# A two-layer hybrid encoder on one core: both directions of the delta rule in one step with unscaled keys, the decay tables moved to the v and q convolutions, and the inversion's columns on one engine

## The chip, the core and the metric

One Trainium2 core: TensorE (PE in the profile) multiplies matrices, VectorE (DVE), ScalarE (ACT) and GpSimd (POOL) work on rows, and SyncE's queue (SP) issues nearly all DMAs. Everything is float32. The metric is the device time of one execution in microseconds; lower is better.

## The reference, cut to what matters

Two layers act on 1024 tokens of width 1024. Each layer normalises the tokens, projects them with one matrix of 3376 columns, runs three mixers (gated linear attention, the gated delta rule, cross-attention into a memory of 256 tokens), gates them, and projects back. The change is about the delta rule: 4 heads of width 96, chunks of 64 tokens, 16 chunks, once from left to right and once from right to left with gates of its own; the two results are added.

```python
def _gated_delta_chunked(q, k, v, g, beta):
    gc = jnp.cumsum(g, axis=-1)
    diff = gc[..., :, None] - gc[..., None, :]
    decay = jnp.where(incl, jnp.exp(jnp.where(incl, diff, 0.0)), 0.0)
    kk = jnp.einsum('bhncd,bhnsd->bhncs', k, k)
    a_strict = jnp.where(strict, kk * decay * beta[..., :, None], 0.0)
    t_mat = a_strict + jnp.eye(c, dtype=jnp.float32)
    rhs = jnp.concatenate([v * beta[..., None], k * (beta * jnp.exp(gc))[..., None]], axis=-1)
    sol = lax.linalg.triangular_solve(t_mat, rhs, left_side=True, lower=True, unit_diagonal=True)
    u, w = sol[..., :dv], sol[..., dv:]
    qk = jnp.where(incl, jnp.einsum('bhncd,bhnsd->bhncs', q, k) * decay, 0.0)
    q_dec = q * jnp.exp(gc)[..., None]
    k_to_end = k * jnp.exp(gc[..., -1:] - gc)[..., None]
    chunk_decay = jnp.exp(gc[..., -1])
    def step(s, inp):
        u_c, w_c, q_c, qk_c, k_c, dec_c = inp
        v_new = u_c - jnp.einsum('bhcd,bhdv->bhcv', w_c, s)
        o = jnp.einsum('bhcd,bhdv->bhcv', q_c, s) + jnp.einsum('bhcs,bhsv->bhcv', qk_c, v_new)
        s = dec_c[..., None, None] * s + jnp.einsum('bhcd,bhcv->bhdv', k_c, v_new)
        return s, o
```

With M for the inverse of `t_mat` (with beta folded in), u is M·v and w is M·(exp(gc)·k). So v_new = u − w·S can also be had as M·(v − exp(gc)·(k·S)); the change rests on that identity.

## The kernel before, in words

A layer has three phases. **phase_norm** normalises eight tiles of 128 tokens, transposes them, and multiplies the first columns of the in-projection. **phase_proj** multiplies the others, tile by tile of 128 output columns ("dense": pieces of 6 matmuls `mm<-Hh,wh` and the like, 128x512, on numbers split into a high and a low part), and starts the delta rule with what comes out: three k convolutions, then three v, then three q (`conv_sink`, four 128x1024 multiply-adds each on DVE, line 535), L2 norms, transposes back, the decay tables N (`decays`, per head: a subtraction on POOL, a minimum on DVE, an exponential on ACT), the products q·k and k·k (`phase_a`), and the inverse M (`invert`: a column-by-column elimination of 32x32 blocks, in columns 0 to 29 on DVE and in columns 30 and 31, as X2, on POOL). Dense pieces are pulled in between (`pull`, `upto`).

**phase_mix** runs the recurrence (`chain`), and after each of its yields lets `filler` issue other work for some nanoseconds of a budget (FILL): the gates and states of the linear attention (`gla_pre`, PE tile `x`), what is left of dense, units of the mixers (`x`, `ga`, `gb`), loads of the output weights (`load_wout`: `wor`, split on ACT and DVE at line 1522), and output tiles.

Before, the chain prepares each tile of two chunks per direction: it scales keys twice on POOL (`ke`, `kend`), builds block-diagonal copies of M on ACT (`Mb`), forms u and w with 8 matmuls (PE tile `pt`) and evacuates both. A chunk step then takes 4 matmuls for w·S and q·S together (`cp<-S,wq`, M=128), DVE's `vn`, 4 matmuls for the state (`R<-vn,kend`), DVE's addition to `S·dec` (POOL), and the outputs (`cp<-vn,qkt`, both directions in turn), which ACT copies out and POOL adds. The backward direction runs one piece behind the forward one. The scaled queries are made in phase_proj (`row`, POOL, lines of phase_proj) and stored in `qd_d`.

PE's instructions are pinned to the order of the code. The other engines' order is a scheduler's, and each of them works through its list in that order, so an instruction that waits holds back all behind it.

## Time and profile before

| | us |
|---|---|
| median of three runs (lowest, highest) | 1391.71 (1391.15, 1397.26) |
| the profiled execution, its own time | 1387.57 |
| its span, first to last instruction | 1385.8 |
| PE busy | 1260.7 (91%) |
| DVE busy | 814.8 (59%) |
| ACT busy | 655.5 (47%) |
| POOL busy | 549.6 (40%) |
| mean granted TensorE clock | 0.965 of full speed |

The profiled execution has 1.8 us outside its span, and the median of the runs lies 4.1 us above it. A fp32 matmul is two records in the trace, so "x8" in a row of the chain is four matmuls. Where a row names a helper's line (84, 87, 90, 98, 101), go by the tile: all matmuls have line 98, all DVE tensor-tensor operations line 87. The stage of the chain lies at 353 to 583 us in layer 0 and at 1041 to 1272 us in layer 1; the convolutions are at 85 to 245 and 765 to 925, the inversions at 262 to 350 and 942 to 1040.

### The profile page before, as it was taken

To read this page: it belongs to the slowest core of one execution; us is meant where nothing else is said; L and a number is where in the kernel's file an instruction comes from. 1 tells how busy PE (TensorE), PEld (TensorE's weight loads), DVE (VectorE), ACT (ScalarE), POOL (GpSimd) and SP (SyncE) were. 2 spreads that over 40 slices of the span, in tenths; PEclk is the share of its full clock that TensorE was granted. 3 is DMA by queue.
4 is the path that set the end of the run, shared out by engine and by line. 5 is a ranking of instruction groups with operands and counts; after the bars stand their busy time and mean duration, and the time that the engine had idled before them with its cause. 6 is when DMAs were issued, how large, how long until landed. Compare 5 with 4: busy or idle time off the path is not lost. (4 is left out here: it accounts for less than half of the span.)

```text
span 1385.8 us, 24239 instructions
## 1 busy us (share of the span) xinstructions
PE 1260.7 (91%) x9482; PEld 1047.5 (76%) x9482; DVE 814.8 (59%) x1163; ACT 655.5 (47%) x1373; POOL 549.6 (40%) x579
## 2 busy tenths in 40 slices
PE   6998799987999988999999988996978998999997
PEld 5986688776777777887788766884767787778886
DVE  5336855498377557356272578455865784564553
ACT  5335564162766655233262545531637675543432
POOL 4026434576534544211310454444854445432111
PEclk9999999999999999999999999998999999999999
DMA  7161234752686865244652413257427776642532
GB/s 223 57 134 35 74 91 130 245 157 69 187 242 197 236 192 144 81 145 125 188 169 66 107 46 106 61 158 221 136 66 225 210 229 203 205 130 80 161 103 106
DMA packets 247857, 198.99 MB, mean 144 GB/s; under 512 B 68032, under 2 KB 215936, under 8 KB 247744
## 3 DMA queue, kind: packets, MB, share of 16 engines
q1 hardware_dynamic: 245584, 189.59, 47.2%
q10 hardware_dynamic: 2016, 7.34, 1.5%
q8 instruction: 75, 1.23, 0.4%
q0 software_dynamic: 144, 0.52, 0.1%
q14 instruction: 38, 0.31, 0.1%
HBM read 138.82 MB, written 58.59 MB: 142 GB/s over the span
## 5 line engine op out<-in xcount | busy, mean ns | idle before, releaser
L98 PE MATMUL mm<-Hh,wh 128*128 128x512 f32 x736 | 311.8, 424 | 31.7 <-ACT acc L84 15.9
L98 PE MATMUL mm<-Hh,wl 128*128 128x512 f32 x736 | 295.9, 402 | 0.0
L98 PE MATMUL mm<-Hl,wh 128*128 128x512 f32 x736 | 295.6, 402 | 0.0
L90 POOL TENSOR_TENSOR wl<-wr,wh 128x1024 fp32r<-128x1024 f32 x46 | 119.4, 2596 | 211.0 <-ACT wh L84 188.3
L98 PEld LDWEIGHTS mm<-Hh,wh 128*128 128x128 f32 x736 | 143.5, 195 | 66.7 <-ACT acc L84 19.3
L535 DVE SCALAR_TENSOR_TENSOR acc<-pad,convw,acc 128x1024 f32<-128x1024 f32 x72 | 139.9, 1943 | 66.4 <-ACT acc L84 63.8
L98 PEld LDWEIGHTS mm<-Hh,wl 128*128 128x128 f32 x736 | 143.2, 195 | 32.3
L98 PE MATMUL mm<-wo,oh 128*128 128x512 f32 x512 | 167.1, 407 | 0.2 <-DVE xr L87 0.2
L98 PEld LDWEIGHTS mm<-Hl,wh 128*128 128x128 f32 x736 | 144.2, 196 | 26.0
L90 POOL TENSOR_TENSOR ol<-z,oh 128x512 fp32r<-128x512 f32 x32 | 41.2, 1286 | 163.6 <-ACT oh L84 161.4
L98 PEld LDWEIGHTS mm<-wo,oh 128*128 128x128 f32 x512 | 90.3, 189 | 17.8 <-issue 0.8
L98 PE MATMUL mm<-wo,ol 128*128 128x512 f32 x256 | 101.2, 395 | 0.0
L90 POOL TENSOR_TENSOR S<-S,dec 96x384 f32<-96x384 f32 x56 | 55.5, 991 | 87.4 <-DVE S L87 66.9
L90 POOL TENSOR_TENSOR acc<-acc,pad 128x1024 f32<-128x1024 f32 x18 | 45.6, 2531 | 107.8 <-ACT pad L84 107.8
L84 ACT ACTIVATE wh<-wr 128x1024 fp32r<-128x1024 f32 x46 | 48.4, 1053 | 74.8 <-PE mm L98 66.2
L98 PEld LDWEIGHTS cp<-S,wq 96*128 96x128 f32 x480 | 62.7, 197 | 14.9 <-ACT oa L84 6.4
L98 PE MATMUL cp<-S,wq 96*128 96x96 f32 x480 | 65.1, 280 | 9.2 <-ACT oa L84 5.5
L84 ACT ACTIVATE oh<-z 128x512 fp32r<-128x512 f32 x32 | 20.2, 632 | 80.4 <-DVE z L87 80.3
L87 DVE TENSOR_TENSOR vn<-u,cp 64x384 f32<-64x384 f32 x60 | 33.0, 550 | 40.9 <-PE cp L98 33.4
L98 PEld LDWEIGHTS mm<-wo,ol 128*128 128x128 f32 x256 | 48.1, 188 | 11.5
L90 POOL TENSOR_TENSOR sp<-sp,sg 128x512 f32<-128x512 f32 x32 | 45.3, 1417 | 28.8 <-ACT sg L84 17.6
L90 POOL TENSOR_TENSOR row<-row,qT 96x1024 f32<-96x1024 f32 x16 | 38.0, 2383 | 44.0 <-DMA row<-row_d 29.3
(311 smaller groups left out, 2652.1 us busy)
## 6 DMA issues: line engine op xcount, KB each, us to landing
wr<-in_w_in_dram SPq DMA_DIRECT2D x46, 512.0 KB, 4.0
kv<-kv_d SPq DMA_DIRECT2D x32, 384.0 KB, 4.4
zT<-sp SPq DMA_DIRECT2D x32, 256.0 KB, 2.4
ge_d<-qe SPq DMA_DIRECT2D x32, 256.0 KB, 3.7
wor<-in_w_out_dram SPq DMA_DIRECT2D x16, 512.0 KB, 4.6
gqk<-ge_d SPq DMA_DIRECT2D x16, 512.0 KB, 4.0
z<-zT SPq DMA_DIRECT2D x16, 512.0 KB, 4.5
row<-row_d SPq DMA_DIRECT2D x16, 384.0 KB, 6.3
```

The lines of the kernel that those rows point to most:

```text
L84: return self.nc.scalar.activation(out, in_, func, **kw)
L87: return self.nc.vector.tensor_tensor(out, a, b, op=op)
L90: return self.nc.gpsimd.tensor_tensor(out, a, b, op=op)
L98: return self.pin(self.nc.tensor.matmul(*args, **kw))
L535: nc.vector.scalar_tensor_tensor(acc, pad[:, j:j + T], self.convw[:, f, j:j + 1], acc, op0=ALU.mult, op1=ALU.add)
```

## The change

The recurrence takes the same chunk step of both directions at once. A step loads keys and queries 96 wide by 64 tokens (`kq`), a broadcast row of exp(gc) (`row`), keys and values in token rows (`kv`) and the q·k block (`qk`), two steps ahead, in 8 DMAs. It multiplies the unscaled keys and the scaled queries with S (8 matmuls each, 64 output rows a piece), forms X = v − exp(gc)·(k·S) on DVE in four operations, multiplies M by X (8 matmuls, 64x64), copies the result out (`vn`, ACT) and scales it for the state (`ve`, DVE), multiplies it by the unscaled keys (`R`, 8 matmuls) and adds. Outputs are copied by ACT in the first half of the steps and added by DVE from PSUM in the second. `ke`, `kend`, `Mb`, u, w, their evacuations and the store `qd_d` are gone; queries are scaled per step on POOL (96x2x256). Three of the four decay tables move from the k to the v and q convolutions. All 32 columns of the inversion are on DVE. Constants of the fill change, and `left` counts what dense has left in place of an estimate.

```diff
-FILL = 1200
-FILL2 = 1200
-FILLW = 1200
-FILL3 = 1200
+FILL = 1950
+FILL2 = 1950
+FILLW = 1950
+FILL3 = 1950
-PRE_D = 24
+PRE_D = 32
-INV = 6000
-DC0 = 0
-CUT = 30
+INV = 9000
-DEN0 = 3
+DEN0 = 6
...
@@ phase_proj
-        self.qd_d = self.DR.tile([2, HD, 4, T], F32, tag="qdd", name="qd_d")
+        self.kq_d = self.DR.tile([HD, 2, 4, T], F32, tag="kqd", name="kq_d")
...
             self.conv_t(3 + i, k_tok[:, :, i * 128:i * 128 + 128])
-            if i >= DC0:
-                next(dec, None)
...
                     self.back_t(k_tok, h, kT[h])
+                    nc.sync.dma_start(self.kq_d[:, 0, h], kT[h])
...
             self.conv_t(i, q_tok[:, :, i * 128:i * 128 + 128])
-        for _ in dec:
-            pass
+            next(dec, None)
...
             self.back_t(q_tok, h, qT[:, h, :])
-            for d in range(2):
-                row = ST.tile([P, T], F32, tag="acc", name="row", bufs=3)[0:HD]
-                nc.sync.dma_start(row.rearrange("p (t c) -> p t c", t=NT),
-                                  self.row_d[:, d * 4 + h].unsqueeze(0).to_broadcast([HD, NT, P]))
-                self.ptt(row, row, qT[:, h, :], ALU.mult)
-                nc.sync.dma_start(self.qd_d[d, :, h], row)
+            nc.sync.dma_start(self.kq_d[:, 1, h], qT[:, h, :])
@@ invert
-            self.ptt(tv, U[:, :, 0:j, j:j + 1].to_broadcast(sh), X2[:, :, j:j + 1, c0:].to_broadcast(sh), ALU.mult)
-            self.ptt(X2[:, :, 0:j, c0:], X2[:, :, 0:j, c0:], tv, ALU.subtract)
-        for j in range(CUT - 1, 0, -1):
-            w = CUT - j
+            w = 32 - j
...
-        self.act(X[:, :, :, CUT:], X2)
@@ phase_mix, filler
-        closePX = self.psum(cp=2, R=1, pt=1, x=2)
+        closePX = self.psum(cp=2, R=2, x=2)
...
-        left = (23 - self.tiles) * 8 - 2
+        left = self.left
...
-            while busy and done < units * left // MIXN:
+            while busy and (done < units * left // MIXN or units >= MIXU):
@@ chain
+    def chain_load(self, MP, n):
+        kv = MP.tile([P, 2, 4, HD], F32, tag="kv", name="kv", bufs=3)
+        kq = MP.tile([HD, 2, 2, 4, 64], F32, tag="kq", name="kq", bufs=3)
+        row = MP.tile([HD, 2, 4, 64], F32, tag="row", name="row", bufs=2)
+        qk = MP.tile([P, 4, 64], F32, tag="qk", name="qkt", bufs=3)
+        for d in range(2):
+            t, f, r = self.place(d, n)
+            cs = slice(t * 128 + f * 64, t * 128 + f * 64 + 64)
+            nc.sync.dma_start(kq[:, d].rearrange("p e h c -> p (e h) c"),
+                              self.kq_d[:, :, :, cs].rearrange("p e h c -> p (e h) c"))
+            nc.sync.dma_start(row[:, d], self.row_d[t, d * 4:d * 4 + 4, f * 64:f * 64 + 64]
+                              .unsqueeze(0).to_broadcast([HD, 4, 64]))
+            nc.sync.dma_start(kv[r].rearrange("p k h d -> p k (h d)"), self.kv_d[:, t, r].rearrange("k p c -> p k c"))
+            nc.sync.dma_start(qk[r], self.qkd[:, r, t, d, :].rearrange("h p c -> p h c"))
...
+            if n:
+                ks = self.ps("cp", [P, 4, HD])
+                for e, to in ((0, ks), (1, o)):
+                    for h in range(4):
+                        for d in range(2):
+                            self.mat(to[at[d][2], h, :], p["kq"][:, d, e, h, :], S[d][:, h, :],
+                                     start=h == 0, stop=e == 0 and h == 3, skip_group_check=True)
+                    if e == 0:
+                        X = MP.tile([P, 4, HD], F32, tag="X", name="X", bufs=1)
+                        for h in range(4):
+                            self.nc.vector.scalar_tensor_tensor(X[:, h, :], ks[:, h, :], neg[:, n, h:h + 1], x[:, h, :],
+                                                                op0=ALU.mult, op1=ALU.add)
+                        x = X
+                if n < N2 - 1:
+                    for d in range(2):
+                        new[d] = MP.tile([HD, 4, HD], F32, tag=f"S{d}", name=f"S{d}", bufs=2)
+                        dec = self.dec[0:HD, at[d][1], at[d][0], d * 4:d * 4 + 4]
+                        self.ptt(new[d], S[d], dec.unsqueeze(2).to_broadcast([HD, 4, HD]), ALU.mult)
+                yield
+            pv = self.ps("R", [P, 4, HD])
+            for h in range(4):
+                for d, (t, f, r) in enumerate(at):
+                    self.mat(pv[r, h, :], self.M[d][r, h, t, :], x[r, h, :], start=True, stop=True)
+            vn = MP.tile([P, 4, HD], F32, tag="vn", name="vn", bufs=1)
+            self.act(vn, pv)
+            ve = MP.tile([P, 4, HD], F32, tag="ve", name="ve", bufs=1)
+            self.tt(ve, pv, end[:, n].unsqueeze(2).to_broadcast([P, 4, HD]), ALU.mult)
+            if n + 1 < N2:
+                self.chain_scale(n + 1, loads[n + 1])
+            yield
+            if n < N2 - 1:
+                R = [self.ps("R", [P, 4, HD]) for _ in range(2)]
+                for h in range(4):
+                    for d, (t, f, r) in enumerate(at):
+                        self.mat(R[d][0:HD, h, :], p["kv"][r, 0, h, :], ve[r, h, :], start=True, stop=True)
...
+                        self.tt(new[d], R[d][0:HD], new[d], ALU.add)
+            for h in range(4):
+                for d, (t, f, r) in enumerate(at):
+                    self.mat(o[r, h, :], p["qk"][r, h, :], vn[r, h, :],
+                             start=n == 0 and h == 0, stop=h == 3, skip_group_check=True)
...
+            if n + 2 < N2:
+                loads[n + 2] = self.chain_load(MP, n + 2)
+            yield
```

How this moves instructions is seen at three places. The first is PE in layer 0, within the chain, while dense pieces are still there. Before (`R` is the state update of one direction, `pt` the w unit, `x` a transpose for the linear attention, `cp<-vn,qkt` the outputs of both):

```order
L98 MATMUL mm<-Hl_106,wh 128x512
L98 MATMUL mm<-Hh_105,wl 128x512
L98 MATMUL R<-vn,kend 96x96 x4
L98 MATMUL pt<-Mb_3165,ke 96x128 x4
L101 MATMUL x<-ident,qe 128x128 x4
L98 MATMUL R<-vn,kend 96x96 x4
L98 MATMUL cp<-vn,qkt 64x96 x8
L98 MATMUL pt<-kv,Mb_3166 128x96 x4
L98 MATMUL mm<-Hh_107,wh 128x512
```

After, at the same dense piece:

```order
L96 MATMUL mm<-Hl_106,wh 128x512
L96 MATMUL mm<-Hh_105,wl 128x512
L96 MATMUL R<-ve,kv 96x96 x8
L96 MATMUL cp<-vn,qkt 64x96 x8
L99 MATMUL x<-ident,qe 128x128 x4
L96 MATMUL mm<-Hh_107,wh 128x512
L96 MATMUL mm<-Hl_108,wh 128x512
L96 MATMUL mm<-Hh_107,wl 128x512
L96 MATMUL mm<-Hh_107,wh 128x512
L96 MATMUL mm<-Hl_108,wh 128x512
L96 MATMUL mm<-Hh_107,wl 128x512
L96 MATMUL cp<-S_3296,kq 64x96
```

The two state updates stand in one group, the `pt` units are gone, and between the update and the next product with S stand the outputs and other work.

The second is DVE beside the three q convolutions of layer 0 (`acc` are the multiply-adds, `N` the minimum of a decay table, `tok` an evacuation). Before:

```order
L535 SCALAR_TENSOR_TENSOR acc<-pad,convw,acc 128x1024 x3
L115 COPY v_t<-tr 128x512
L535 SCALAR_TENSOR_TENSOR acc<-pad,convw,acc 128x1024 x4
L115 COPY tok<-tr 128x4x128
L535 SCALAR_TENSOR_TENSOR acc<-pad,convw,acc 128x1024 x4
L115 COPY tok<-tr 128x4x128 x2
```

After:

```order
L535 SCALAR_TENSOR_TENSOR acc<-pad,convw,acc 128x1024 x3
L85 TENSOR_TENSOR N<-N,cap 128x1024
L535 SCALAR_TENSOR_TENSOR acc<-pad,convw,acc 128x1024
L113 COPY tok<-tr 128x4x128
L535 SCALAR_TENSOR_TENSOR acc<-pad,convw,acc 128x1024 x2
L85 TENSOR_TENSOR N<-N,cap 128x1024
L535 SCALAR_TENSOR_TENSOR acc<-pad,convw,acc 128x1024
L113 COPY tok<-tr 128x4x128
L535 SCALAR_TENSOR_TENSOR acc<-pad,convw,acc 128x1024
L85 TENSOR_TENSOR N<-N,cap 128x1024
L113 COPY tok<-tr 128x4x128
```

Three minima now lie among the multiply-adds of this stage, where none stood; the three that stood among those of the k convolutions are gone from there, and one stays at the second v convolution as before.

The third is DVE around the output weights in layer 0, after the last dense piece (`wo` is a split of output weights, `U` a state of the linear attention, `S` a state of the delta rule). Before, two splits at a time stand between steps of the chain:

```order
L87 TENSOR_TENSOR S_4328<-R,S_4328 96x384
L1522 SCALAR_TENSOR_TENSOR wo_4906<-wor,onw,wo_4906 128x512
L1522 SCALAR_TENSOR_TENSOR wo_4909<-wor,onw,wo_4909 128x512
L87 TENSOR_TENSOR S_4411<-R,S_4411 96x384
L87 TENSOR_TENSOR vn<-u,cp 64x384 x2
```

After:

```order
L1411 SCALAR_TENSOR_TENSOR wo_5319<-wor_5135,onw,wo_5319 128x512
L1198 SCALAR_TENSOR_TENSOR U<-U,ff,x 128x96
L1411 SCALAR_TENSOR_TENSOR wo_5141<-wor_5133,onw,wo_5141 128x512
L1411 SCALAR_TENSOR_TENSOR wo_5306<-wor_5133,onw,wo_5306 128x512
L1411 SCALAR_TENSOR_TENSOR wo_5393<-wor_5137,onw,wo_5393 128x512
L1411 SCALAR_TENSOR_TENSOR wo_5322<-wor_5137,onw,wo_5322 128x512
L1198 SCALAR_TENSOR_TENSOR U<-U,ff,x 128x96 x4
L85 TENSOR_TENSOR S_4400<-R,S_4400 96x384
```

Eight splits now stand between a step's `ve` and its two additions to S (the piece shows the last five of them); on PE no dense or mixer matmul stands between that step's groups and the next product with S.

## Rows read from the trace of the kernel before

**Rows 1.** The page, part 1: busy time, share and instructions of each engine.

```profile
PE 1260.7 (91%) x9482; PEld 1047.5 (76%) x9482; DVE 814.8 (59%) x1163; ACT 655.5 (47%) x1373; POOL 549.6 (40%) x579
```

**Rows 2.** Windows, core 0: stretch, length, busy engines, PEclk, DMA share, GB/s.

```profile
353.00:467.00 114.00, 105.57 (x942) 87.89 (x941) 79.39 (x137) 77.59 (x165) 49.63 (x51) 0.99 0.79 223
467.00:583.00 116.00, 107.15 (x1035) 91.31 (x1034) 59.10 (x105) 52.45 (x124) 52.48 (x56) 0.99 0.52 149
...
88.00:98.00 10.00, 10.00 (x46) 8.29 (x45) 6.67 (x4) 4.08 (x7) 2.40 (x1) 1.00 0.89 152
...
1094.00:1104.00 10.00, 10.00 (x79) 8.18 (x80) 7.73 (x16) 5.84 (x13) 3.68 (x4) 1.00 1.01 294
```

**Rows 3.** Chain of waits, layer 1: start, us, engine, tile, line, records.

```profile
1049.56 1.37 PE mm L98 x6
...
1083.70 0.87 PE cp L98 x8
1084.57 0.89 PE pt L98 x8
...
1087.09 0.85 PE R L98 x8
1087.94 1.04 PE pt L98 x8
...
1090.26 0.81 PE cp L98 x16
...
1279.28 1.09 PE ga L98 x16
...
1285.04 1.47 PE gb L98 x32
```

**Rows 4.** PE timeline at the inversion: start, us, operation, shape, idle before.

```profile
348.99 1.27 PE L98 MATMUL cp<-FT,N 32*32 32x32 f32 x127
```

**Rows 5.** PE's waits, 85 to 175 us: us, times, longest.

```profile
PE mm L98 <- ACT acc L84: 7.6, 4, 3.5
```

**Rows 6.** PE's waits, 245 to 352 us.

```profile
PE mm L98 <- ACT sg L84: 6.2, 3, 2.8
PE cp L98 <- DVE FT L745: 5.5, 1, 5.5
```

**Rows 7.** PE's waits, 925 to 1040 us.

```profile
PE mm L98 <- ACT sg L84: 9.6, 2, 7.2
PE cp L98 <- DVE N L87: 6.5, 1, 6.5
```

**Rows 8.** DVE and POOL by form: count, busy us, mean ns, idle before.

```profile
L535 DVE SCALAR_TENSOR_TENSOR acc<-pad,convw,acc 128x1024 f32<-128x1024 f32 x72 | 139.9, 1943 | 66.4 <-ACT acc L84 63.8 <-POOL acc L90 0.4
L87 DVE TENSOR_TENSOR vn<-u,cp 64x384 f32<-64x384 f32 x60 | 33.0, 550 | 40.9 <-PE cp L98 33.4 <-POOL oa L90 7.1
L1522 DVE SCALAR_TENSOR_TENSOR wo<-wor,onw,wo 128x512 fp32r<-128x512 f32 x32 | 24.8, 797 | 21.6 <-ACT wo L84 21.6
L1309 DVE SCALAR_TENSOR_TENSOR U<-U,ff,x 128x96 f32<-128x96 f32 x56 | 17.2, 308 | 4.0 <-PE x L98 2.6
L87 DVE TENSOR_TENSOR N<-N,cap 128x1024 f32<-128x1024 f32 x8 | 9.8, 1220 | 3.7 <-POOL N L90 3.7
...
L90 POOL TENSOR_TENSOR row<-row,qT 96x1024 f32<-96x1024 f32 x16 | 38.0, 2383 | 44.0 <-DMA row<-row_d 29.3 <-DVE qT L115 7.5 <-PE mm L98 7.2
L90 POOL TENSOR_TENSOR N<-N,gB 128x1024 f32<-128x1024 f32 x8 | 22.5, 2818 | 0.0
```

**Rows 9.** DVE timeline, inversions of both layers: start, us, operation, shape, idle before.

```profile
283.81 0.27 DVE L87 TENSOR_TENSOR tmp<-U,X 128x58 f32<-128x58 f32 x1
...
325.27 0.22 DVE L87 TENSOR_TENSOR X<-X,tmp 128x58 f32<-128x58 f32 x1
328.74 1.97 DVE L745 STREAM_TRANSPOSE FT<-X 128x1024 f32<-128x1024 f32 x1 [3.25 <-ACT X L84]
...
942.49 0.69 DVE L87 TENSOR_TENSOR qk<-cp,N 128x512 f32<-128x512 f32 x1 [10.41 <-DMA qkd<-qk]
```

More of the change, by code (lines that the diff above doesn't have):

```diff
@@ L1037, in chain, with place @@
+        return neg, end
+    def place(self, d, n):
+        t, f = (n // 2, n % 2) if d == 0 else (NT - 1 - n // 2, 1 - n % 2)
+        return t, f, slice(f * 64, f * 64 + 64)
     def chain(self, MP):
         S = [None, None]
-        self.nMb = 0
-        self.vn = MP.tile([P, 4, HD], F32, name="vn")
-        self.Mb = [MP.tile([P, 4, P], F32, name=f"Mb{i}") for i in range(2)]
-        for m in self.Mb:
-            self.nc.gpsimd.memset(m, 0.0)
-        preps = {}
-        units = []
-        arrived = set()
```

206 lines of the change are left out of this document (35 added, 171 removed).

## The prediction

> **What bounds the kernel now.** I read the busy times first. PE is busy 1260.7 of 1385.8 us, and no other engine reaches two thirds of the span [rows 1]. So time can be won in two ways: by taking work off PE, or by taking away some of the 125 us in which it stands. Next come the windows of the recurrence in layer 0, whose PE columns give 105.57 of 114 us and 107.15 of 116 us [rows 2]. There PE is the pace, and its instructions, not a latency, set the end. The same rows hold a warning in their last columns: in the first of the two stretches DVE is busy 79.39 us and the DMA engines 0.79 of the time, in the second DMA has 0.52. A recurrence that needs more bytes has room in the second stretch and little in the first. PE's waits outside the recurrence come last: near the k convolutions [rows 5] and around the two inversions [rows 6, 7].
>
> **The recurrence's matmuls.** One chunk step of both directions costs before: two products with S (0.87 each), two state updates (0.85 each), the outputs of both (0.81), and, for two tiles in two steps, u and w (0.89 and 1.04) [rows 3]; together 6.2 us. After, none of these is in the trace, so I take the nearest shapes. k·S is 8 matmuls of 64 output rows over 96 columns; 16 such column halves, as `gb`, take 1.47 us, so 8 take 0.74. q·S is another 0.74. M·X is 8 matmuls 64x64, as the outputs before: 0.81. The update with 64 rows is like `ga`, 8 row halves over 128 columns in 1.09; for 96 columns 0.82. The outputs stay at 0.81 [rows 3]. That is 3.9 us. With the first and last steps, which lack some groups, a layer has 95.6 us before and 60.5 after: **−35 a layer, −70 in all**. Bounds: none of the shapes is worse than a group of full size (0.87 to 1.04), which would make it 4.8 us a step and −21 a layer; if pieces of 64 are no cheaper beside dense pieces, that is the end.
>
> **The recurrence's loads.** Counted from the tiles' shapes, a step loads before 704 KB for both directions (keys and values 384, w and q 192, q·k 128) and after 1088 KB, of which 704 KB come in pieces of 64 numbers (256 bytes). Pieces of that size are seen where N is loaded: 152 GB/s at a share of 0.89, so 171 GB/s at most; the mix of the recurrence ran at 223 GB/s at 0.79, so 282, and at 294 at the full share [rows 2]. A step then occupies the queues for 3.95 us (all at 282) to 5.6 us (the small pieces at 171). I take 4.8, halfway, since the new pieces lie beside larger ones. In the first stretch 90 us of transfers lie, about 25 of them loads of the recurrence and 65 others. All of the output weights' first half and more are now loaded ahead of its end, five more pieces of 512 KB (9 us), and ten steps take 48. So the DMA needs some 122 us, while PE would need about 90.6 us of work and 12 of other delays, 103. Loads run two steps ahead and some slip into the second stretch, where the DMA has room, so about half of the gap is paid: **+10 a layer**; bounds 0 and +27.
>
> **What the fill leaves uncovered.** The order shows that dense ends near the tenth step. One step then has nothing between its groups, and on DVE eight splits of output weights stand between its `ve` and its additions to S: 8 × 0.80 = 6.4 us [rows 8], held back by ACT's half of each split as well. Only mixer units, each of which waits for ACT or DVE in between, stand between the groups of the last five steps. I price the bare step at 7 us and the five at 1 us each: **+12 a layer**; bounds +4 (splits taken early) and +20.
>
> **Waits of the steps with fill.** Before X there are 0.74 (q·S) and 6 dense matmuls of 1.37 [rows 3] on PE against four DVE operations of 0.31 [rows 8]; before the update, 1.37 and often an `x` unit against one DVE operation of about 0.55; before the next k·S the outputs, 0.81, and 1.37 against two additions of 0.55 [rows 8]. Each is covered, by 0.5 us or more, as long as DVE comes to them at once. I take nothing here; what it costs when the cover is gone is the last rival. POOL gives up `ke`, `kend` and the output additions and gets the scaling of queries; it is busy 49.63 of 114 us [rows 2], and I cost it at nothing.
>
> **Decay tables.** A table takes 2.82 us of POOL and 1.22 us of DVE [rows 8]. Beside the k convolutions DVE is what PE waits for: 7.6 us for `acc` in four waits [rows 5], with DVE's multiply-adds at 1.94 us each while POOL works beside them [rows 8]. Three tables less are 3.7 us of DVE and 8.5 of POOL there; I take **−6.5 a layer**, between −3.7 (DVE's part only) and −10.8 (7.6 and the wait of the same stretch for the first v, 3.2). Beside the q convolutions no wait is recorded before, but the slack is small, and two tables more are 2.4 us of DVE and 5.6 of POOL: **+3 a layer**, bounds 0 and +6.
>
> **Row products and stores.** Eight loads, eight POOL operations of 2.38 us [rows 8] and eight stores of 384 KB go; eight stores of the same size stay for `kq_d`. In layer 1 DVE's `qk` waits 10.41 us for the store of the previous one, queued behind these transfers on SP [rows 9], and PE waits for N 6.5 us [rows 7]. With the loads gone I take −2.7 in layer 0 and −8 in layer 1, **−11**; bounds −4 and −14.
>
> **The inversion.** POOL's 62 small operations go, and DVE does 62 on up to 512 columns where it did 58 on up to 450. Its loop lies between 283.81 and 325.49 us [rows 9]; growing by the columns it would gain 4.7 us, and lose the waits that POOL's small operations cause. Behind it, FT waited 3.25 us for ACT's copy of POOL's columns [rows 9], which is gone. By these, FT comes 1 to 4 us earlier. Besides, 12 dense matmuls are pulled ahead of the product with FT, 2.8 us. PE's wait for FT was 5.5 and 4.3 us [rows 6, 7], so it goes: **−10 in both layers**; bounds +4 (the loop grows by more than it saves) and −12.
>
> **The sum.** −70 + 20 + 24 − 13 + 6 − 11 − 10 = −54 us. Against the profiled execution, 1387.6, that is 1333.6; the median of the runs lies 4.1 us above that, so **1338**.
>
> **Rivals.** *First: neither DMA nor fill costs.* Loads are ahead by two steps, and mixers fill well. Then the 44 us are not paid: 1294. For it speaks that PE is the pace in both stretches before [rows 2]; against it, 0.79 of DMA share with 54% more bytes a step. Chance 0.16. *Second: the loads are the pace.* At 5.6 us a step and with both other ends, the recurrence pays about 43 us a layer instead of 22: 1380. For it speaks the 171 GB/s, against it the free half of the second stretch [rows 2]. Chance 0.15. *Third: the two halves of a bank go one after the other.* M·X and the outputs now write both directions' halves into one PSUM tile, from two halves of rows; before, the outputs had a tile for each direction. If such pairs ran in series, 0.8 us more twice a step would be 51 us: 1389. The trace speaks against it: in the inversion 64 matmuls 32x32 from four strips of rows into one tile take 1.27 us [rows 4], where a third of a `gb` pair's 0.18 us each, in series, would be 3.9. Chance 0.04. The Trainium skill, TensorEngine Tiling (Array Packing), section Restrictions and Gotchas, says that different row tiles cannot access one PSUM bank at the same time, which is this rival; the 1.27 us here do not agree with that.
>
> *Fourth, the slower side: in step, the hand-overs are in the open.* Before, one direction's matmuls hid the other's additions; in step both wait at the same three points, 96 in all (3 a step, 16 steps, 2 layers). Each goes through DVE, whose list also holds the linear attention and the splits, and which is busy 0.70 of the first stretch before [rows 2]; an operation of 0.8 to 1.0 us ahead in its list delays PE by that, and ACT and POOL have hand-overs behind. Over the forecast, a mean of 0.56 us more for each brings the kernel back to its time before, and 1.0 us more gives 1434. For it speaks that `vn` before had nothing to do with the other direction and PE lost little; against it, the dense pieces between all three points up to the tenth step. Chance 0.12.
>
> **How the numbers follow.** The forecast has 0.53 and by itself 1308 to 1368 (its unknown terms by about half of their bounds). The range goes down to the first rival and up to the third, 1290 to 1390; outside it are the fourth and the lower tail of the first. I can tell a change from none by 0.5%, about 7 us. Faster by more than that: the forecast, the first and two thirds of the second rival, 0.80; within it 0.08; slower 0.12.
>
> **What would show it.** In the profile after: groups of 8 at 0.74 to 0.82 us (else the first term is wrong); the recurrence's stage about 17 us a layer shorter, with the DMA share of its first part at 0.9 or more and waits for `kq` or `row` if the loads bind; one wait of 5 us or more for S in the bare step; fewer waits for `acc` at 85 to 175 us, some new ones for `acc` or `tok` in the q stage; no wait for FT. Waits of 1 us for X, `ve` or S in most steps would be the fourth rival, and a time over 1390 would make the prediction wrong.

## The result, and the profile after

| | before | after |
|---|---|---|
| median of 20 runs each (lowest, highest) | 1391.17 (1379.15, 1404.30) us | 1403.87 (1394.31, 1413.17) us |
| ratio to before, 95% interval | | 1.0094 [1.0077, 1.0112] |
| profiled execution (span) | 1387.57 (1385.8) us | 1413.17 (1411.5) us |
| mean granted TensorE clock | 0.965 | 0.926 |

The kernel is 0.9% slower; the forecast was 1338, in a range of 1290 to 1390. The profiled execution of after is the slowest of its 20, so the two profiles differ by 25.7 us where the medians differ by 12.7. Where a sum is made below it is made between the profiles, and half of it may be that execution's own.

The page, part 1 and the count of DMA packets, answers [rows 1]:

```profile
PE 1217.5 (86%) x9962; PEld 997.3 (71%) x9962; DVE 830.3 (59%) x1263; ACT 616.9 (44%) x1291; POOL 397.8 (28%) x363
...
DMA packets 299318, 205.37 MB, mean 146 GB/s; under 512 B 144064, under 2 KB 267392, under 8 KB 299200
```

PE has 43 us less to do and stands 69 us longer (194 for 125). Before, the page counted 68032 packets under 512 bytes. The two stretches of the recurrence, in the columns of [rows 2]:

```profile
353.00:467.00 114.00, 96.41 (x993) 74.63 (x992) 65.19 (x132) 64.83 (x138) 41.95 (x37) 0.90 0.94 222
467.00:583.00 116.00, 76.60 (x950) 63.91 (x949) 63.01 (x130) 41.90 (x105) 28.39 (x30) 0.79 0.73 187
```

PE no longer sets the pace in either, its clock has fallen from 0.99, and the DMA engines need 0.94 of the time to move what ran at the same 222 GB/s with 0.79. PE's waits over the whole span (us in total, times, longest):

```profile
PE x L96 <- DMA gv<-vg: 41.7, 6, 11.9
PE R L96 <- DVE ve L85: 24.0, 10, 5.3
PE tr L99 <- POOL acc L88: 23.9, 4, 9.0
PE cp L96 <- DVE FT L724: 21.1, 4, 7.3
```

Four waits of 21 to 42 us each are new or have grown. Only the second is a hand-over of the new recurrence. Marks on PE's row (the last transpose behind a convolution, the first and last product of `phase_a`, M done, the last chain step, the last output) cut both profiles into the same stretches. In microseconds, after less before:

| stretch | layer 0 | layer 1 | forecast, both layers together |
|---|---|---|---|
| to the last v transpose (k and v convolutions) | −6.8 | −6.1 | −13 |
| q convolutions | +9.2 | +9.2 | +6 |
| from there to the first product of `phase_a` | +2.3 | +1.8 | 0 |
| `phase_a` | −2.8 | −8.2 | −11 |
| inversion, with 12 more dense matmuls in each | −1.5 | −3.5 | −4.4 |
| recurrence (225.6 and 228.5 before) | +20.9 | +7.3 | −31.6 |
| behind the recurrence | +1.7 | +2.4 | 0 |

The forecast of the lines for the inversion and the recurrence is written with the 2.8 us of dense that the change takes from each recurrence into each inversion (−10 + 5.6, and −70 + 20 + 24 − 5.6). The sum of the misses is 80 us, and 60 of them lie in the recurrence.

The matmuls' own price came out as predicted. PE in layer 0, at one step with dense between its groups (start, us, shape, idle before):

```profile
441.28 1.54 PE L96 MATMUL cp<-S,kq 96*64 96x96 f32 x32
...
444.73 0.88 PE L96 MATMUL R<-X,M 64*64 64x96 f32 x16
...
448.44 0.92 PE L96 MATMUL R<-ve,kv 64*96 64x96 f32 x16 [0.44 <-DVE ve L85]
449.29 0.88 PE L96 MATMUL cp<-vn,qkt 64*64 64x96 f32 x16
```

These durations add up to 4.2 us a step. But each group overlaps the next by some 0.07 us (448.44 and 0.92 against 449.29), and from start to start the four take the 3.9 us of the forecast, against 6.2 in [rows 3]. Fifty microseconds on, where dense has run out, the same groups read:

```profile
488.38 0.88 PE L96 MATMUL x<-gv,kt 128*64 128x96 f32 x16 [3.58 <-DMA gv<-vg]
...
501.75 1.55 PE L96 MATMUL x<-gv,kt 128*64 128x96 f32 x16 [11.91 <-DMA gv<-vg]
503.23 1.60 PE L96 MATMUL R<-ve,kv 64*96 64x96 f32 x16
...
510.06 0.88 PE L96 MATMUL R<-X,M 64*64 64x96 f32 x16
515.95 1.60 PE L96 MATMUL R<-ve,kv 64*96 64x96 f32 x16 [5.01 <-DVE ve L85]
```

Behind a wait of 11.91 us the groups take 1.55 to 1.60: the granted clock is at 1.2 GHz. In the next step M·X takes 0.88, so it is at 2.4 GHz again, and behind the wait of 5.01 us the groups are back at 1.60. The recurrence's windows (from M to its last step; columns as above) sum this up, of before:

```profile
356.75:582.37 225.62, 208.34 (x1836) 175.62 (x1835) 138.49 (x241) 128.20 (x285) 100.35 (x101) 0.98 0.65 185
1043.61:1272.14 228.53, 211.62 (x1835) 178.49 (x1835) 136.21 (x241) 129.41 (x289) 97.60 (x99) 0.96 0.64 184
```

and of after:

```profile
357.22:603.71 246.49, 189.12 (x2053) 151.09 (x2053) 139.06 (x284) 107.03 (x244) 72.95 (x70) 0.85 0.79 195
1059.84:1295.64 235.80, 185.37 (x2053) 147.70 (x2053) 138.61 (x284) 107.35 (x245) 71.12 (x69) 0.87 0.78 206
```

PE is busy 374.5 us in both layers, where the forecast left 344.4 (420.0 − 70 − 5.6), and idle 107.8, where it left 78.2 (34.2 + 44). So of the 60 us half are busy time and half are waits. The busy half is the clock: by the clock records of the traces PE is busy 86.6 us of both layers at the lower clock, for 22.2 before, and work at half speed makes 32 us of that difference.

### The profile page after: what moved, and what is told of

Read it like the earlier page. It is cut to its first block, busy times and chain, and to the rows that moved or that the text cites. A ratio compares the mean times of both kernels' runs of the same rounds, so it can differ in the third digit from the quotient of the medians.

```text
span 1411.5 us, 25212 instructions
## 1 busy us (share of the span) xinstructions
PE 1217.5 (86%) x9962; PEld 997.3 (71%) x9962; DVE 830.3 (59%) x1263; ACT 616.9 (44%) x1291; POOL 397.8 (28%) x363
## 2 busy tenths in 40 slices
DMA packets 299318, 205.37 MB, mean 146 GB/s; under 512 B 144064, under 2 KB 267392, under 8 KB 299200
## 4 chain that ended last, share of the span: by engine, by line
PE 45%; DVE 23%; DMA 11%; ACT 8%; issue 6%; SPq 5%; POOL 1%; DVEq 0%; ACTq 0%; POOLq 0%
PE mm L96 28%; DVE acc L535 7%; PE cp L96 5%; PE tr L99 3%; PE x L96 3%; DVE tmp L85 3%; DVE X L85 3%; ACT pad L82 3%; PE R L96 2%; DVE U L707 2%; PE gb L96 1%; DMA wr<-in_w_in_dram 1%; DMA gv<-vg 1%; DMA kv<-kv_d 1%; ACT wh L82 1%
## 5 line engine op out<-in xcount | busy, mean ns | idle before, releaser
L88 POOL TENSOR_TENSOR wl<-wr,wh 128x1024 fp32r<-128x1024 f32 x46 | 116.4, 2531 | 316.4 <-ACT wh L82 304.1
L535 DVE SCALAR_TENSOR_TENSOR acc<-pad,convw,acc 128x1024 f32<-128x1024 f32 x72 | 133.5, 1857 | 69.9 <-ACT acc L82 55.5
L88 POOL TENSOR_TENSOR S<-S,dec 96x384 f32<-96x384 f32 x56 | 51.4, 934 | 95.6 <-DVE S L85 91.6
L88 POOL TENSOR_TENSOR kq<-kq,row 96x512 f32<-96x512 f32 x30 | 39.4, 1312 | 129.7 <-DMA row<-row_d 56.5
L85 DVE TENSOR_TENSOR ve<-R,end 128x384 f32<-128x384 f32 x32 | 17.6, 551 | 83.0 <-ACT vn L82 82.9
L96 PE MATMUL cp<-S,kq 96*64 96x96 f32 x960 | 55.3, 266 | 8.4 <-DVE oa L85 2.9
L96 PEld LDWEIGHTS cp<-S,kq 96*64 96x64 f32 x960 | 46.8, 149 | 19.9 <-issue 4.2
L96 PE MATMUL x<-gv,kt 128*64 128x96 f32 x256 | 18.8, 304 | 45.6 <-DMA gv<-vg 41.7
```

What stands on the lines that cost most here:

```text
L85: return self.nc.vector.tensor_tensor(out, a, b, op=op)
L88: return self.nc.gpsimd.tensor_tensor(out, a, b, op=op)
L96: return self.pin(self.nc.tensor.matmul(*args, **kw))
L535: nc.vector.scalar_tensor_tensor(acc, pad[:, j:j + T], self.convw[:, f, j:j + 1], acc, op0=ALU.mult, op1=ALU.add)
```

## The experiments

Each is a change to the kernel after, unless it says otherwise. "Recurrence" is the sum of the two windows above, 454.2 before and 482.3 after, in that kernel's profile. How far to trust it is shown by e11 and e15: their recurrence is the code of before, word for word, and took 467.1 and 461.5. A difference under 13 us in that column says nothing. Ratios are to the kernel before on the same chip, with a 95% interval. The medians of different runs come from chips on which the kernel before has 1388.5 to 1391.2 us, so a difference of two medians is good to about 3 us.

**Are the loads the cause?** In e1_loads_once steps from the fourth on reuse the first three steps' data; e3_half_bytes loads half of each tile from there on.

```diff
+        if n >= 3:
+            return dict(kv=kv, kq=kq, row=row, qk=qk)
```

> The recurrence loads its operands for the first three steps only and uses these again, so the results are of no use; all other work stays. Three theories for the 25 us that the recurrence's stage in the changed kernel takes more than I forecast. Issue: SP's queue, at some 0.6 us a DMA and 8 a step, is full (50 of 57 us) and holds back the linear attention's loads (PE waits 41.7 us for gv). Transfer: the 16 DMA engines are full (share 0.94 in the first part). Hand-overs: the loads don't matter, PE stands at X, ve and S. Issue and transfer both expect the waits for gv, gqk, kv, row (53 us) to shrink to under 10 and a time of about 1355 (0.975 of before). Hand-overs expects 1390 to 1405.

```diff
+                nc.sync.dma_start(kq[:, d, n % 2], self.kq_d[:, n % 2, :, cs])
+            nc.sync.dma_start(row[:, d, hs], self.row_d[t, d * 4:d * 4 + hw, f * 64:f * 64 + 64]
```

> Each of the 8 loads of a step stays, but from the fourth step on it brings half of its bytes (two heads of four, or keys and queries in turn); the results are of no use. Issue expects no change: 1398 to 1410, gv waits still over 30 us. Transfer expects the DMA share of the first part to fall from 0.94 to about 0.75 and the waits for gv to fall under 20: 1375 to 1390. Hand-overs expects no change.

Measured: e1 1369.4 us, 0.9871 [0.9823, 0.9918], recurrence 440.5; e3 1390.9 us, 1.0008 [0.9977, 1.0039], recurrence 464.6. The windows of e1:

```profile
357.21:575.06 217.85, 180.00 (x2053) 142.82 (x2053) 137.95 (x284) 106.53 (x244) 77.32 (x70) 0.92 0.56 154
1029.40:1252.09 222.69, 183.95 (x2053) 145.62 (x2053) 137.95 (x284) 106.49 (x245) 77.59 (x68) 0.91 0.54 153
```

The loads cost 34.5 us of the time (31 by the ratios) and 41.8 of the recurrence; the forecast had 20. e1's time lies between what the theories expected (about 1355, or 1390 and more). Half of the bytes, with as many DMAs as after, gives back 13.0 us (e3).

The two layers differ. In layer 0 the loads cost 28.6 us (246.49 less 217.85), over the forecast's upper bound of 27; in layer 1 they cost 13.1 (235.80 less 222.69), near the 10 that it took. From share times length of the same windows, an estimate of the loads' price follows: the 13 steps that e1 does not load took 72.7 us of the engines in layer 0 and 63.7 in layer 1, so 5.6 and 4.9 us a step. Counted from the packets in the trace of after, those of 256 bytes moved at 176 GB/s at the full share in layer 0 and at 214 in layer 1; in e4, e5, e7, e13 and e16, which load the same pieces, it is 168 to 179 and 212 to 219. Why the layers differ is not known.

Without the loads the recurrence is still 38 us over the forecast's 402.6 (454.2 − 70 − 5.6 + 24).

**Is it the issuing queue?** SP issues all eight loads of a step and those of `gv` behind them, and the chain of waits of after has `kv<-kv_d` at 8.49 us and `gv<-vg` at 7.66. e2_act_queue gives four of the eight to ACT's queue, e4_gv_act gives it `gv`.

```diff
-            nc.sync.dma_start(kq[:, d].rearrange("p e h c -> p (e h) c"),
+            nc.scalar.dma_start(kq[:, d].rearrange("p e h c -> p (e h) c"),
...
-            nc.sync.dma_start(v.rearrange("p t a b -> p t (a b)"),
+            nc.scalar.dma_start(v.rearrange("p t a b -> p t (a b)"),
```

> The loads of keys and queries (kq) and of the row are issued by ACT instead of SP: 4 of the 8 a step, same bytes. Issue expects SP's queue to have some 2.6 us a step back, the waits for gv to fall from 41.7 us to under 20, and 1375 to 1390. Transfer expects no change, 1398 to 1410. Hand-overs expects no change or a little worse, since ACT is delayed.

> Only the linear attention's gv loads (8 a layer) are issued by ACT; the recurrence's loads are as they were. Issue expects that gv no longer stands behind the recurrence's loads on SP: its wait falls from 41.7 to under 15 us, 1380 to 1392. Transfer expects the wait to stay over 25 us, as a load takes as long to land. Hand-overs expects the wait to turn into others, with a time of 1395 to 1405.

Measured: e2 1412.2 us, 1.0179 [1.0127, 1.0232], recurrence 488.5; e4 1409.5 us, 1.0158 [1.0118, 1.0199], recurrence 478.8. PE's wait for `gv` in e2, and in e4:

```profile
PE x L96 <- DMA gv<-vg: 23.0, 5, 7.8
```

```profile
PE x L96 <- DMA gv<-vg: 11.9, 3, 6.8
```

The named wait shrinks in both (from 41.7), and the time doesn't: others of 6 to 28 us, `ve` in e2 (28.3), `U` and `qe` in e4, take its place. So relief of SP's queue alone brought nothing; in e2 PE also waits longer for what ACT makes (`ge`, 10.5 us for 3.4). That SP's issuing has no part in the loss is not shown by these two, but e3 and e10 (below) move the time with as many DMAs on SP as in after.

**Is it the pieces?** e8_tile_loads loads `kq` and `row` once for two steps, in pieces of 512 bytes where they were 256; the bytes are the same, the DMAs of two steps are 12 for 16. e10_pieces_128 keeps bytes and DMAs of after and lays `kq_d` out so that a piece has 128 bytes. e12_layouts is e9 (below) with layouts in DRAM that give pieces of 1 to 4 KB.

```diff
-            cs = slice(t * 128 + f * 64, t * 128 + f * 64 + 64)
+            cs = slice(t * 128, t * 128 + 128)
+            if n % 2 == 0:
...
-        self.kq_d = self.DR.tile([HD, 2, 4, T], F32, tag="kqd", name="kq_d")
+        self.kq_d = self.DR.tile([HD, 2, 4, 2, T // 2], F32, tag="kqd", name="kq_d")
...
-        self.kq_d = self.DR.tile([HD, 2, 4, T], F32, tag="kqd", name="kq_d")
+        self.kq_d = self.DR.tile([HD, NT, 2, 4, 128], F32, tag="kqd", name="kq_d")
```

> Keys, queries and rows are loaded for two steps at once: same bytes, pieces of 512 instead of 256 bytes, 12 DMAs in two steps instead of 16. Half of all bytes gone gave 13 us. If small pieces are what fills the DMA engines, this gives as much or more: 1384 to 1392 and a DMA share of the first part under 0.88. If bytes alone count, the time stays at 1398 to 1408.

> The changed kernel with keys and queries loaded in pieces of 128 instead of 256 bytes: same bytes, same DMAs, 1536 more pieces a step (tokens come in another order, so the results are of no use). If the number of small pieces sets the stage, it grows as it shrank when 1152 pieces a step went: 1420 to 1435 and a higher DMA share in the second stretch. If bytes count, 1400 to 1408.

> The first of these four, with the stored keys, queries, q-k blocks laid out so that a load finds a direction's whole tile in one piece (kq 4 KB, row 2 KB, qkt 1 KB; the small pieces move to the stores, in stages with DMA room). If small pieces are what fills the DMA engines, the recurrence's stage shrinks by another 5 to 10 us a layer: 1340 to 1355. If 512 bytes were already enough, no change against the first: 1358 to 1368. If the stores now hold up the first products, the stage with phase_a grows.

| `kq` in pieces of | packets under 512 B | time, us | ratio | recurrence |
|---|---|---|---|---|
| 128 bytes (e10) | 193216 | 1434.8 | 1.0312 [1.0221, 1.0403] | 506.6 |
| 256 bytes (after) | 144064 | 1403.9 | 1.0094 [1.0077, 1.0112] | 482.3 |
| 512 bytes (e8) | 69312 | 1385.2 | 0.9977 [0.9947, 1.0006] | 455.6 |
| loads of the first three steps only (e1) | 67520 | 1369.4 | 0.9871 [0.9823, 0.9918] | 440.5 |

The first recurrence window of e10, then that of e8 with its stretch from 353 us:

```profile
354.94:612.77 257.83, 190.65 (x2053) 152.50 (x2053) 138.50 (x284) 107.67 (x244) 72.00 (x71) 0.85 0.82 186
```

```profile
353.32:584.92 231.60, 185.87 (x2053) 147.32 (x2053) 141.22 (x284) 106.81 (x244) 75.65 (x85) 0.90 0.82 207
...
353.00:467.00 114.00, 94.70 (x918) 72.28 (x904) 73.32 (x138) 67.42 (x145) 42.19 (x46) 0.94 1.01 250
```

With the same bytes, pieces of 512 in place of 256 give back 18.7 us (16 by the ratios), over half of what all loads cost, and pieces of 128 take 30.9 more. e8 also issues fewer DMAs and loads earlier, and what that is worth was not tested by itself; e10, with the DMAs of after, changes the pieces. e8's expected share under 0.88 did not come: the engines are at 1.01 there and move 250 GB/s, so 248 at the full share, for 236 in after (222 at 0.94) and 282 before. Larger pieces add nothing that can be seen: e12, from which 10 to 20 us less than e9 were expected if they counted, has 1377.3 us, 0.9891 [0.9822, 0.9960], recurrence 462.7, against e9's 1383.4, 0.9943 [0.9911, 0.9975] and 454.0.

**Is it dense running out?** e7_pred24 puts back the constants of before that keep dense for longer; e14_once_pred24 does the same in e1.

```diff
-PRE_D = 32
+PRE_D = 24
...
-DEN0 = 6
+DEN0 = 3
```

> PRE_D and DEN0 as before (24 and 3): fewer dense pieces beside the linear attention's first part, so some are left for later steps. If the waits at the end of dense (11.9 and 10.1 us for gv, 5 us for ve in the bare step) come from dense running out, they shrink and the clock stays up there: 1380 to 1394. If the loads are the pace, the waits move ahead and the time stays at 1398 to 1408.

> Loads of the first three steps only (as in the run that was at 1369), and PRE_D and DEN0 as before (24 and 3), so that dense pieces last longer. If the 38 us that the recurrence's two stages still lack of my forecast without loads come from dense running out (bare step, mixer units by themselves), the stage falls by 10 us or more: 1350 to 1362. If they lie at hand-overs of every step, 1366 to 1374.

Measured: e7 1398.0 us, 1.0066 [1.0033, 1.0098], recurrence 482.2; e14 1377.9 us, 0.9910 [0.9878, 0.9943], recurrence 458.4 against 440.5 without that edit. In e7 the wait for `gv` falls to 8.2 us, and `ge` (20.3), `As` (14.3) and `pT` (14.2) come up. e7's interval overlaps that of after, and e14 is no better than e1, so more fill at the end does not help, with loads or without.

**Is it the clock?** e13_busy_work puts 4 and 12 matmuls of 128x512 on data at hand before the last two `x<-gv,kt` of a layer, where PE waited 3.58 and 11.91 us in layer 0 (what they compute is read by nobody).

```diff
+            for _ in range({6: 4, 7: 12}.get(groups.index((pr, d, hf)), 0)):
+                self.mat(self.mm(), self.M[0][:, 0, 0:2, :].rearrange("p t c -> p (t c)"),
```

> The changed kernel with 4 and 12 extra 128x512 matmuls, whose results nobody reads, ahead of the linear attention's last two state products in each layer, where PE waits 2.8 to 3.6 and 10 to 12 us for gv; nothing else differs. Clock: the granted clock falls while PE stands there, and what follows runs at half rate; the extra work fills the waits, the matmuls behind them take 0.8 instead of 1.6 us, and the stage of both layers loses 4 to 15 us: 1388 to 1400. Waits alone: the extra work is hidden or costs what exceeds the waits, 1402 to 1412, and PE's busy time grows by the extra work alone.

PE of e13 at that place in layer 0:

```profile
486.48 10.47 PE L96 MATMUL mm<-M,M 128*128 128x512 f32 x24
497.80 0.88 PE L96 MATMUL x<-gv,kt 128*64 128x96 f32 x16 [0.86 <-DMA gv<-vg]
498.61 0.92 PE L96 MATMUL R<-ve,kv 64*96 64x96 f32 x16
...
512.31 0.55 PE L96 MATMUL x<-kh,xq 128*128 128x256 f32 x1 [5.04 <-DMA xq<-xq]
```

The groups behind take 0.88 and 0.92 where they took 1.55 and 1.60, and 14 us on PE stands 5.04 us for another load. Time 1403.6 us, 1.0098 [1.0069, 1.0128], recurrence 480.3: as after. So at these places the low clock follows the wait and costs nothing that shows in the time. In layer 0 what comes next is late by a load anyway; in layer 1 PE's groups are back at 1.55 us behind a wait of 1.24, and no load of that size stands there.

**The hand-over to `ve`.** DVE's `ve` (product and state's decay) waits for ACT's `vn`, not for PE. The group on the page, with DVE's idle time before it:

```profile
L85 DVE TENSOR_TENSOR ve<-R,end 128x384 f32<-128x384 f32 x32 | 17.6, 551 | 83.0 <-ACT vn L82 82.9
```

Both read the same PSUM tile, `vn` is issued first, and `ve` is put behind it, though neither changes that tile. The three longest of PE's waits for `ve`, 15 of the 24 us, begin with a load. The wait of 5.01 us above and that of 4.86 at the same place in layer 1 come from ACT's list, where `vn` stands behind `kh` of the cross-attention (ACT, then DVE):

```profile
513.87 1.06 ACT L82 ACTIVATE kh<-kraw 128x1024 fp32r<-128x1024 f32 x1 [7.37 <-DMA kraw<-mkv]
514.83 0.47 ACT L82 ACTIVATE vn<-R 128x384 f32<-128x384 f32 x1
```

```profile
515.33 0.56 DVE L85 TENSOR_TENSOR ve<-R,end 128x384 f32<-128x384 f32 x1 [5.21 <-ACT vn L82]
```

The wait of 5.30 us comes from DVE's own list, where `ve` stands behind `qe` of the linear attention:

```profile
420.92 2.78 DVE L85 TENSOR_TENSOR qe<-qkin,ge 128x512 f32<-128x512 f32 x1 [2.44 <-DMA qkin<-qg]
423.63 0.68 DVE L85 TENSOR_TENSOR qe<-qkin,gm 128x512 f32<-128x512 f32 x1
424.23 0.54 DVE L85 TENSOR_TENSOR ve<-R,end 128x384 f32<-128x384 f32 x1
```

e16_ve_first exchanges the two statements; e17_e9_ve_first and e18_once_ve_first do it in e9 and e1.

```diff
-            vn = MP.tile([P, 4, HD], F32, tag="vn", name="vn", bufs=1)
-            self.act(vn, pv)
             ve = MP.tile([P, 4, HD], F32, tag="ve", name="ve", bufs=1)
             self.tt(ve, pv, end[:, n].unsqueeze(2).to_broadcast([P, 4, HD]), ALU.mult)
+            vn = MP.tile([P, 4, HD], F32, tag="vn", name="vn", bufs=1)
+            self.act(vn, pv)
```

> The changed kernel with two instructions of a step exchanged: DVE's ve before ACT's vn. Both read the product of M and X, and in the changed kernel ve waits for vn in all 32 steps (82.9 us of DVE's idle time is put down to that), so the way to the state goes through ACT's list as well. If this hand-over costs, PE's waits for ve fall from 24 us to under 12 and the stage of both layers shrinks by 8 to 20 us: 1384 to 1396. If the loads' time covers it, no change: 1400 to 1408.

> The run with loads for two steps, late decay tables and columns on POOL (1383), with the same exchange. Where the loads are lighter, the exchange should show more: 1362 to 1374 if the hand-over costs, 1380 to 1386 if not.

> The run with loads of the first three steps only (1369), with the same exchange. PE's waits for ve were 9.8 us there. If the hand-over through ACT is part of the 38 us that are missing without loads, 1352 to 1363; if not, 1366 to 1373.

Measured: e16 1397.2 us, 1.0042 [1.0014, 1.0069], 6.7 us under after, and the wait for `ve` is no more among its longest; e17 1376.3 us, 0.9897 [0.9842, 0.9951], 7 us under e9, with intervals that overlap; e18 1372.0 us, 0.9862 [0.9814, 0.9910], no better than e1. PE's waits in e16:

```profile
PE x L96 <- DMA gv<-vg: 40.5, 6, 8.8
PE tr L99 <- POOL acc L88: 24.0, 4, 9.0
PE cp L96 <- DVE FT L724: 21.7, 4, 7.3
```

The exchange is worth about 7 us with the loads of after, and nothing that shows without loads. That fits the rows above: without loads (e1) the longest wait for `ve` is 1.5 us.

**Tables and columns.** e5_stages_back puts the tables and the inversion's columns back as before; e11_stages_alone does to the kernel before only what e5 undoes; e6_decays_late moves the three later tables behind the q convolutions; e9_tile_late_pool is e8 with POOL's columns and the tables behind the q norms; e15_before_late does the latter to the kernel before.

```diff
@@ e5 (k convolutions, then the inversion; e11 has - for +)
+            next(dec, None)
...
+            self.ptt(X2[:, :, 0:j, c0:], X2[:, :, 0:j, c0:], tv, ALU.subtract)
...
+        for j in range(CUT - 1, 0, -1):
@@ e6 (q convolutions)
-            next(dec, None)
+        for _ in dec:
+            pass
         self.l2norm(ST, q_tok, HD ** -0.5)
@@ e9, e15
         self.pull(8 * U)
+        for _ in dec:
+            pass
```

> Undoes the two parts outside the recurrence: three decay tables beside the k convolutions again, and the inversion's columns 30 and 31 on POOL again. By the marks in the trace the changed kernel won 6 to 7 us a layer by the last v transpose, lost 9.2 at the last q convolution, and won 1.5 to 3.5 in the inversion. If the two parts stand by themselves, the marks go back by these numbers and the time stays within 6 us of the changed kernel's 1404. If the tables' place also set what the recurrence does, the stage from the inverse to the last chain step moves by over 5 us.

> The kernel before with the two parts outside the recurrence as in the changed kernel: decay tables beside v and q convolutions, all columns on DVE. If these parts act alone as the marks show (k and v stage -13, q stage +18, columns +4), the time is 1395 to 1402. If they are worth what I forecast (-13 +6 and nothing for the columns), 1381 to 1386.

> The two decay tables that lie among the q convolutions are issued behind the last of them. If the q stage's 9.2 us a layer come from minima on DVE and subtractions on POOL that hold up the multiply-adds, they go and nothing else grows: 1384 to 1390. If the tables only find the next place where they are waited for (q norms, first products with N), the stage up to the last product with N stays as long: 1400 to 1406.

> Three things together: the loads of two steps at once (512-byte pieces, 1385 by itself), the inversion's two columns back on POOL (1.6 and 2.4 us by the marks), and the two late decay tables issued behind the q norms, where POOL is idle. If each is worth what the marks show (18, 4 and 2 times 9 us), the time is 1358 to 1368, and the wait for acc at the last q convolution is gone. If the tables are waited for there too, 1376 to 1385.

> The kernel before, and of the change only that three decay tables leave the k convolutions; the two that would lie among the q convolutions are issued behind the q norms. If the k and v stage's gain of 6 to 7 us a layer is real and the tables cost nothing there, 1376 to 1382; if the first products with N wait for them, 1386 to 1392.

| | time, us | ratio | in the trace |
|---|---|---|---|
| e5 | 1391.8 | 1.0017 [0.9988, 1.0046] | last q convolution of layer 0: 11.8 us, as before |
| e11 | 1409.9 | 1.0119 [1.0045, 1.0193] | marks ahead of the recurrence +4.1 and +6.9 |
| e6 | 1398.7 | 1.0085 [1.0051, 1.0119] | last q convolution of layer 0: 21.0 us, as after |
| e9 | 1383.4 | 0.9943 [0.9911, 0.9975] | PE's waits for `acc` on POOL 14.5 in all, for 23.9 |
| e15 | 1398.2 | 1.0052 [1.0030, 1.0075] | layer 0: −8.6 by the last v transpose, −4.1 by the last q, +1.5 at the start of the recurrence |

Only e9 came out as one of its expectations had it. e5 gave back 12.1 us where a time within 6 us of after was expected, e11 and e15 are slower than either of theirs, and e6 lies between its two.

What the tables cost beside the q convolutions is seen in after's rows there (layer 0; DVE's minimum and the multiply-add behind it, then POOL, then PE):

```profile
208.69 3.42 DVE L85 TENSOR_TENSOR N<-N,cap 128x1024 f32<-128x1024 f32 x1
212.04 2.96 DVE L535 SCALAR_TENSOR_TENSOR acc<-pad,convw,acc 128x1024 f32<-128x1024 f32 x1
...
215.52 1.27 DVE L535 SCALAR_TENSOR_TENSOR acc<-pad,convw,acc 128x1024 f32<-128x1024 f32 x1
```

```profile
207.65 3.38 POOL L88 TENSOR_TENSOR wl<-wr,wh 128x1024 fp32r<-128x1024 f32 x1
210.99 2.92 POOL L88 TENSOR_TENSOR N<-N,gB 128x1024 f32<-128x1024 f32 x1
221.17 2.35 POOL L88 TENSOR_TENSOR wl<-wr,wh 128x1024 fp32r<-128x1024 f32 x1 [7.25 <-ACT wh L82]
223.47 2.33 POOL L88 TENSOR_TENSOR acc<-acc,pad 128x1024 f32<-128x1024 f32 x1
```

```profile
225.86 1.97 PE L99 MATMUL tr<-ident,acc 128*128 128x128 f32 x8 [8.99 <-POOL acc L88]
```

A minimum that takes 1.22 us in [rows 8] takes 3.42 here; POOL splits weights (`wl`) beside it until 211.03. The multiply-add behind it takes 2.96 beside POOL's subtraction, where one with POOL idle takes 1.27. The last convolution's addition stands on POOL behind a split of weights that itself waited 7.25 us for ACT. PE waits 8.99 us for it. In e6 the tables come later in the code, but not in POOL's list: the scheduler still puts two subtractions (3.82 us together) ahead of that addition, and the last convolution stays at 21.0. Taking the tables out of the k convolutions alone, in the kernel before, moves the last v transpose by −8.6 us and makes the kernel slower (e15), so a gain in that stretch is given back behind it.

**What the loss of 12.7 us is made of.** Undoing either of two parts brings the kernel back to its time before. Pieces of 512 bytes do so with the tables and columns left in place (e8, 0.9977). Tables and columns put back do so with the small pieces left in place (e5, 1.0017). By the marks, tables and columns cost 13.7 us: 18.4 in the q convolutions, 4.1 behind them, 4.1 of columns, less the 12.9 won. e11, which makes them alone in the kernel before, agrees in its marks (+11.0 ahead of the recurrence); the rest of its 1.2% lies in a recurrence that it leaves as it was. The two gains do not simply add: e9, which has the larger pieces, POOL's columns and later tables, is at 0.9943. e8 together with e5's place of the tables was not run. So the loss belongs to neither alone.

## Why the prediction was wrong

Three steps failed most. The loads' term priced a step too low in layer 0 and assumed that half of the gap is paid. The matmuls' term assumed that PE keeps its full clock. The decay tables' term priced a table beside the q convolutions by the table's own time only. Term by term:

- **Matmuls, −70: right in price, wrong in the clock.** The groups take 0.77 to 0.92 at the full clock, and M·X at 0.88 speaks against the rival of serial halves. But the term took the 0.99 of [rows 2] along. In the recurrence of after the clock is 0.85 and 0.87, and half the miss there, 30 us, is PE time. At the two places of each layer that e13 fills, the low clock follows a wait and costs nothing that shows; for the rest of the 30 us that is not shown.
- **Loads, +20: right mechanism, half its size.** They cost 41.8 of the recurrence and 34.5 of the time, and time rises with every step to smaller pieces. What failed is the price of a step, 4.8 us, "halfway, since the new pieces lie beside larger ones", and "about half of the gap is paid". In layer 0 a step took some 5.6 us, the term's upper end, and the recurrence paid 28.6, all of the gap at that price. In layer 1 it took 4.9 and paid 13.1, near the forecast's 10. Nor did PE wait for `kq` or `row`, as the prediction would have had it (1.2 us in all for `row`), but for `gv` of the linear attention: 41.7 us, and 14.2 without the loads (e1). e4 and e7 show that the wait goes elsewhere when `gv` comes early.
- **Fill, +24: the cause was wrong.** No wait for S exceeds 2.3 us in the recurrence, so the bare step's splits did not do it. In layer 0 the last of the eight is done on DVE at 499.95, ahead of the update on PE at 503.23, since PE stands 11.91 us for `gv` there. The step behind it stands 5.01 us for `ve` (4.86 in layer 1), from a load that ACT's list waits for. That waits of the forecast's size stand at this end is luck: loads make them, not the missing fill. The other idle time at the end is spread.
- **Hand-overs, nothing: wrong.** "Before the update … one DVE operation of about 0.55" left out that DVE's operation comes behind ACT's copy, and that either can stand behind an operation that waits for a load. PE waited 24.0 us for `ve` in ten places, up to 5.3; e16 prices the order at about 7 us of the time. So the fourth rival was right at one of its three points, far below the 54 us with which it would have decided alone.
- **What stays open.** Without loads the recurrence is 38 us over the forecast: 20 of PE time at the lower clock (364.0 for 344.4) and 18 idle, in many hand-overs of the linear attention, the mixers and the chain; the longest entry of e1's waits in the recurrence is `gv` with 14.2 us in both layers. Taking the `ve` wait away (e18) or keeping dense longer (e14) brought none of it back. What would is not settled, and the 13 us of scatter in that stage are a third of it.
- **Decay tables: −13 came, +6 was +18.** The −13 is no gain by itself: e15, which takes the tables out of the k convolutions and changes nothing else, is slower than before (1.0052). The bound of 6 us a layer in the q convolutions (9.2 measured) priced two tables by their own time. The order shown ahead of the prediction has three minima there, and what the term left out is a minimum beside POOL (3.42 for 1.22) and the list of POOL in which the last addition stands. With the 4 us behind, that is 16 us of the miss.
- **Row products, −11: right** (−2.8 and −8.2).
- **Inversion, −10: about right in size, for a wrong reason.** In layer 0 DVE's loop grew by 4.6 us (46.3, from 282.97 to 329.29, for 41.7 in [rows 9]), about what the columns alone were to cost; the waits for POOL's operations that were to go with them did not come off. That takes all of the 3.25 us that ACT's copy had cost, FT's first transpose starts at 329.33 where [rows 9] had 328.74, and the wait that was to go is 7.33 us, since PE has less to do ahead of it. DVE, then PE:

```profile
282.97 0.98 DVE L85 TENSOR_TENSOR tmp<-U,X 128x62 f32<-128x62 f32 x1
...
329.07 0.22 DVE L85 TENSOR_TENSOR X<-X,tmp 128x62 f32<-128x62 f32 x1
329.33 1.91 DVE L724 STREAM_TRANSPOSE FT<-X 128x1024 f32<-128x1024 f32 x1
```

```profile
338.96 1.92 PE L96 MATMUL cp<-FT,N 32*32 32x32 f32 x124 [7.33 <-DVE FT L724]
```

In layer 1 the loop took 46.5 us for 47.0 before, where one wait of 6.7 us lay in it. With POOL's columns back (e5) the stage is 1.6 and 2.4 us shorter, and the waits for FT are 6.2 us in place of 21.1.

The rivals on the faster side had 0.16 and the slower side 0.12. What happened is a part of the second, a part of the fourth, a clock that no rival had, and q convolutions outside their bounds: several terms of moderate size, nearly all to the same side. Two of the sums do not come out as written: by the stated bounds (27 and 20 us a layer) the second rival is 47 and 1388, not 43 and 1380, and the 90.6 us of PE work in the loads' term are not worked out. The forecast's own range took the unknown terms at half of their bounds, as if they would offset each other.

## What to carry to other kernels

Before a formulation is exchanged for one with fewer matmuls, count its loads by piece size as well as by bytes: here 18.7 us, more than the whole loss, hung on pieces of 256 bytes, and one load for two steps gave them back. Where a copy and a product read the same PSUM tile on two engines, issue first the one that the critical path needs. Ask of every operation on the critical path what stands ahead of it in its engine's list, and whether that waits for a load. With the larger pieces, POOL's columns, tables behind the q norms and `ve` first (e17) the changed recurrence comes to 1376.3 us, 1.0% under the kernel before; e12 stands beside it at 1377.3.

## What the runs showed of the hardware

Pieces of 128, 256 and 512 bytes at the same bytes gave 1434.8, 1403.9 and 1385.2 us; above 512 nothing more could be seen (e12 against e9). The Trainium skill, DMA: Bandwidth & Descriptors, section Specifications, gives 512 bytes as the least transfer for the full rate; the runs agree. A minimum on DVE took 3.42 us where POOL's split of weights ran beside it for 2.3 us, and 1.22 in [rows 8]. And one profile's stage says less than was thought: the same recurrence code, with the same order of loads, took 454.2, 461.5 and 467.1 us in three kernels.
